# Parts of 16, 12 and 16 chunks in the channel mixers, norm blocks split inside the fourth down panel, and one moved set of seven products, in a two-layer hybrid decoder on one Trainium2 core

## The chip, the cores and the metric

The kernel runs on one core of one Trainium2 chip. The metric is the device time of one execution in microseconds (us); lower is better. The core has a matrix engine (TensorE, in the profile PE, its weight loads PEld), a vector engine (VectorE, DVE), a scalar engine (ScalarE, ACT), a general engine (GpSimd, POOL) and an engine for loads and waits (SyncE, SP). Each runs its own instructions in order, and they meet through semaphores. Transfers between main memory and the core's memory are issued by an engine into a queue and land later. TensorE accumulates into eight banks of 128 x 512 fp32.

## The reference: what is computed

256 tokens of width 2048 pass two layers. Each layer is a mixer (layer 0: gated linear attention, layer 1: forgetting attention, "FoX"; both with attention to 256 memory tokens beside it) and then a gated MLP, the channel mixer, with a causal depthwise convolution of width 3:

```python
def conv_ffn(h, w_up, conv_w, conv_b, w_down):      # w_up 2048 x 11264, w_down 5632 x 2048
    u = causal_dwconv(h @ w_up, conv_w, conv_b)
    a, val = split_cols(u, [FFN_HIDDEN, FFN_HIDDEN])
    return (jax.nn.silu(a) * val) @ w_down

for i in range(2):
    if i == 1:
        fk, fv, fc = fox_shared_kv(x, fox_kv_norm, fox_w_kv, fox_b_f)   # rmsnorm(x) @ w_kv
    h = rmsnorm(x, norm_mix[i]);  x = x + mixer_i(h, ...)
    h = rmsnorm(x, norm_ffn[i]);  x = x + conv_ffn(h, ...)
return rmsnorm(x, norm_final)
```

All of it is fp32. The FoX keys and values are made from the residual stream after layer 0's channel mixer, so the step after that channel mixer is a norm and a product with the key weights.

## The kernel before

**Products.** Each fp32 operand is held as a high and a low part (fp32r), and a product takes three matmuls: high x high, high x low, low x high. Activations are stored as chunks of 128 features by 256 tokens with both parts. Weights come as units of 128 x 1024 fp32 (512 KB): SP loads a unit into one of four `raw` buffers, ACT casts it to the high part `whi` (L229) and VectorE subtracts to get the low part `wlo` (L230), each with four buffers. A plain unit then costs TensorE twelve matmuls of 512 columns.

**Sets of seven.** In `pair_steps` (L379) two neighbouring chunks k, k+1, two halves of the tokens and two halves of the columns form a 2 x 2 block product. For chosen k it is done with seven products in place of eight (21 matmuls for 24). It needs sums of weight halves (VectorE, L425 to L428; casts at L375 and L376), sums of activations (`token_sums`, tiles `usum` and `dsum`), four more accumulator banks, and afterwards `early`, which adds the shared products to their places.

**The channel mixer** (`ffn`, L1363). The 5632 hidden features are 44 chunks. An up pair makes four of them: 16 units, one per chunk of the input `h`, with one set of seven at unit 6 (`SEVEN_UP`), and in some pairs another at 11 (`SEVEN_MORE`). Its results are scaled, transposed on VectorE, sent to main memory and brought back transposed through GpSimd's queue (`far_away`, L629), and then go through convolution taps on ACT (L1381), additions on VectorE (L1388), silu (L1394), the product (L1401) and the split into high and low part (L513, L514), which give the chunk `m`. `m` is a ring of 20 chunks. After each part of the chunks (`PARTS`) the down panels of that part run: a wide panel for columns 0 to 1023 (f = 0) and one for 1024 to 2047 (f = 2), one unit per chunk; they add into the residual stream x. In the last part only the first panel is wide; the columns from 1024 on are two panels of 512, f = 2 and f = 3 (`panel_tm`, L312, in layer 0, `rows_tm`, L343, in layer 1), two chunks per unit. Below they are the third and the fourth panel.

**Order.** The work behind an up pair waits in a list. After each unit, `tick` gives it a credit (1.3, 1.7 or 2.1), and the steps whose turn has come are issued until the credit is used up: half a credit a tap, one an addition. Results return three ticks after they were sent, and their taps begin eight ticks after. A planner then orders each engine's instructions by a simulated time: what is ready goes, loads and casts with priority over the rest, and `issue_after` sets what an instruction may not come ahead of. So a step written late can stand earlier in an engine's queue.

**After the last part.** When a panel of x is done, `then(f, b)` (L1588) adds up its squares (ACT, L608) and transposes the block (VectorE, L1594); with both token halves there, the block is sent away on GpSimd's queue. `land` (L1572) brings it back with four transfers, and `take` (L1581) splits it with the norm gain into four chunks of the next input, with ACT (L524) and VectorE (L526). In layer 0 these four blocks are the input of the FoX keys, and `fox` (L1132) starts with `two_tm`: six units of key panel 0, six of key panel 1, then the last two of each. Unit u of a key panel reads chunks 2u and 2u + 1, so units 0 and 1 need block 0, units 2 and 3 block 1, and so on. In the code before, the first block is taken at the end of the fourth panel and the others inside the key panels:

```python
for u in (4, 5):
    f2(u)
    then.land()
for u in range(2, 6):
    if u == 5:
        then.land()
        then.take()
    f3(u)
```

In layer 1 `then` (L1653) multiplies x with the gain of the last norm (L1657, `gf`, loaded by SP in `begin`), and `last` (L1659) ends the kernel: it adds the fourth panel to x, computes the root and writes out, for token half 0 and then half 1. Its last weight units are kept in `spare` tiles, so that half 1 needs no second load.

Of the kernel before, what the change touches and what calls it, by code (L numbers as in the profile page):

```python
# [13 lines left out]
F32 = mybir.dt.float32  # L14
# [6 lines left out]
P = 128  # L21
# [8 lines left out]
RANK = 16  # L30
TAU = 16.0
BIG = 1e30
PARTS = ((0, 16), (16, 32), (32, 44))
RING = 20
SEVEN_UP = (6,)
SEVEN_DOWN = (4, 10)
SEVEN_MORE = 11


# [106 lines left out]
def _trunk(ctx: ExitStack, tc: tile.TileContext, xt, xtok, memt, wp, wgu, gns, gfin, cnv, par, msk, out):  # L146
# [196 lines left out]
    def rows_tm(key, src, evac):  # L343

        units = where[key]
        n = units[0][2]
        base = min(min(u[1]) for u in units)
        acc = [pacc.tile([P, 512], F32, name="acc", tag="acc") for _ in range(2)]
        end = len(units) - 1
        ready = {}  # L350

        def step(i, blocks=(0, 1), hold=None):
            if i not in ready:
                ready[i] = split_unit(units[i]) if hold is None else split_apart(units[i], hold)
            for low in range(2):
                for b in blocks:
                    for j, kc in enumerate(units[i][1]):
                        w = ready[i][low]
                        w = w[j] if isinstance(w, list) else w[:, j * n : (j + 1) * n]
                        for part in range(2 - low):  # L360
                            mm = TE.matmul(acc[b][:, :n], src[kc - base][:, part, b * P : (b + 1) * P], w, start=i == low == part == j == 0,  # L361
                                           stop=i == end and low == 1 and j == len(units[i][1]) - 1)
# [769 lines left out]
    def fox(nx, vt, stash):  # L1132
        hk, hq, mix = bufB, bufA, bufB
        with (
# [24 lines left out]
            def query_input(i):  # L1159
                split_turned(hq, i, (*stash, spare[1])[i // 4], "mix1")  # L1160

            two_tm([fk(0), fk(1)], 8, 2, {(0, 0): nx.take, (0, 3): nx.take, (1, 2): nx.row,
                                          (1, 3): lambda: nx.land(spare[1]), (1, 5): nx.take})
            step = fk(2)
            for u in range(8):
# [197 lines left out]
    def ffn(l, nx, h, m, ys, zs, landing, then, pool, temps, last=None, spare=None):  # L1363
        with tc.tile_pool(name=f"ffn{l}", bufs=1) as fp:
# [8 lines left out]
            def held(name, i):  # L1373
                return fp.tile([P, 2, 4, P], F32R, name=name, tag=f"{name}{i}")
# [21 lines left out]
            def gated(j, s):  # L1396

                if s == 0:
                    product[0] = fp.tile([P, 2, T], F32, name="cv", tag="cv")
                    with tc.issue_after(lows[-1].ins):  # L1400
                        V.tensor_tensor(product[0], taps[0][:, :, 0, :], taps[0][:, :, 1, :], ALU.mult)  # L1401
                r = product[0]
                with tc.issue_after(lows[-1].ins):
                    split(m, (j + s) % RING, r[:, s, :])
                    if s and j < PARTS[-1][0] and j % 16 in SEVEN_DOWN:
                        sums[j] = held("dsum", j % 16)
                        token_sums(r, sums[j])

            product = [None]
# [89 lines left out]
            for p, (lo, hi) in enumerate(PARTS[:-1]):  # L1499
# [10 lines left out]
                more = {SEVEN_MORE: input_sums(SEVEN_MORE, "dsum", SEVEN_DOWN[0])}  # L1510
            lo, hi = PARTS[-1]
            while done < hi:
                drive(up_pair(done, more), 1.3 if done + 4 < hi else 1.7)
                more = {}
                done += 4
            p = len(PARTS) - 1
            src = [m[c % RING] for c in range(lo, hi)]
            wide = down_pair(l, p, 0, src, {}, 0, pool, lambda: (temps(0), temps(1)), then)

            def third(b, a):  # L1520
                add_to(2)(b, a)
# [2 lines left out]
            if l:  # L1524
                f2, f3 = [rows_tm(("down", l, p, f), src, evac) for f, evac in ((2, third), (3, last))]
            else:
                for f, k in zip((2, 3), SEVEN_DOWN):
                    then.rooms[f] = lambda k=k: fp.tile([P, 4, 4, 2, 32], F32, name="tblk", tag=f"dsum{k}")
                f2 = panel_tm(("down", l, p, 2), src, third)
                f3 = panel_tm(("down", l, p, 3), src, lambda b, a: (add_to(3)(b, a), then(3, b)))  # L1530
            for k in range(8):
                next(wide)
                tick(1.7)
            getattr(then, "begin", int)()
            for step, n in ((f2, 4), (f3, 2)):
                for u in range(n):
                    step(u)
                    tick(2.1)
            if l:
# [66 lines left out]
    n = gla(nx)  # L1606
# [159 lines left out]
```

## Time and profile before

| | us |
|---|---|
| median of 3 runs | 2234.88 (2233.97 to 2235.39) |
| the profiled execution | 2235.35 |
| its span | 2233.6 |
| TensorE busy in it | 2212.0 |
| VectorE busy | 1779.7 |
| ACT busy | 1418.3 |
| GpSimd busy | 136.1 |

The granted clock of TensorE in that execution is 0.998 of full speed. The lengths of matmuls in a profile overlap, since they are pipelined, so the pace of TensorE is read from start to start. In a row of a timeline stand the start, the length, the engine, the line, the operation, what it writes and reads, the count of merged instructions, and in brackets the idle time of the engine before it with what ended that. Names of tiles can be those of an earlier owner of the same place: for layer 0 `B` is the input of the up pairs and later of the FoX keys, and `mix`, `A` and `more...` are chunks of m.

### The profile page before, as it was taken

What the parts mean: (1) busy time and instruction counts of PE and PEld (TensorE: products, weight loads), DVE (VectorE), ACT (ScalarE), POOL (GpSimd) and SP (SyncE); (2) the same over time, 40 slices, a digit from 0 to 9 for tenths busy, and PEclk for the clock granted to TensorE, in tenths of its full rate; (3) what the DMA queues carried; (4) which work ended last, traced back from release to release, by engine and by line L of the source; (5) the groups of instructions that cost most, each with busy time, mean ns of one, the idle gap of its engine ahead of it and who ended that gap; (6) DMA issues with size and microseconds to landing.
All of it is one profiled execution on the core that took longest, in us unless ns stands there. A gap on an engine that the chain in (4) does not pass through costs nothing.

```text
span 2233.6 us, 30036 instructions
## 1 busy us (share of the span) xinstructions
PE 2212.0 (99%) x10323; PEld 1852.3 (83%) x10323; DVE 1779.7 (80%) x2638; ACT 1418.3 (63%) x2255; POOL 136.1 (6%) x257
## 2 busy tenths in 40 slices
PE   9999999999999999999999999999999999999998
PEld 7888888888788888888877998888878888888886
DVE  7768977688887888888867559668898788978876
ACT  6655664556786567665665455455787647676466
POOL 0000000001100001100111000000100000110010
PEclk9999999999999999999999999999999999999999
DMA  9867667877678567766677867777677757765674
GB/s 349 248 223 226 192 188 243 249 240 239 227 237 255 193 220 250 222 229 212 227 236 248 236 200 243 225 244 242 220 234 238 244 198 234 258 228 209 224 236 165
DMA packets 165633, 515.47 MB, mean 231 GB/s; under 512 B 20700, under 2 KB 41832, under 8 KB 165480
## 3 DMA queue, kind: packets, MB, share of 16 engines
q1 hardware_dynamic: 148488, 461.36, 63.2%
q0 software_dynamic: 16416, 51.40, 7.6%
q8 instruction: 81, 1.33, 0.2%
q10 hardware_dynamic: 576, 0.79, 0.1%
q14 instruction: 72, 0.59, 0.1%
HBM read 469.68 MB, written 43.79 MB: 230 GB/s over the span
## 4 chain that ended last, share of the span: by engine, by line
PE 91%; ACT 3%; issue 2%; DMA 2%; DVE 0%; POOL 0%; SPq 0%; ACTq 0%; DVEq 0%; POOLq 0%
PE acc L400 27%; PE acc L333 23%; PE ps_s L400 14%; PE ps_o L400 7%; PE ps_t L400 7%; PE acc L305 3%; PE acc L260 3%; PE ps_s L333 2%; DMA fvt<-far 2%; PE acc L258 1%; ACT tap L1381 1%; ACT whi L229 1%; PE acc L361 1%; PE ps_s L1008 0%; ACT whi L375 0%
## 5 line engine op out<-in xcount | busy, mean ns | idle before, releaser
L230 DVE TENSOR_TENSOR wlo<-raw,whi 128x1024 fp32r<-128x1024 f32 (+4 forms) x739 | 874.3, 1193 | 295.6 <-ACT whi L229 278.1
L229 ACT ACTIVATE whi<-raw 128x1024 fp32r<-128x1024 f32 (+4 forms) x739 | 760.9, 1037 | 443.1 <-PE acc L333 157.9
L333 PE MATMUL acc<-whi,B 128*128 128x512 f32 (+3 forms) x1248 | 294.8, 371 | 5.7 <-ACT B L524 5.7
L333 PEld LDWEIGHTS acc<-whi,B 128*128 128x128 f32 x1248 | 227.7, 189 | 34.8 <-ACT B L524 6.5
L375 ACT ACTIVATE whi<-raw 128x1024 fp32r<-128x1024 f32 (+1 forms) x136 | 129.9, 955 | 195.5 <-PE acc L400 71.7
L400 PE MATMUL acc<-whi,B 128*128 128x512 f32 x794 | 203.1, 390 | 1.4 <-ACT whi L229 1.3
L376 DVE TENSOR_TENSOR wlo<-raw,whi 128x1024 fp32r<-128x1024 f32 (+1 forms) x136 | 147.8, 1088 | 69.9 <-ACT whi L375 61.3
L400 PE MATMUL acc<-whi,mix 128*128 128x512 f32 x754 | 192.6, 390 | 1.2 <-ACT whi L229 1.0
L400 PEld LDWEIGHTS acc<-whi,B 128*128 128x128 f32 x794 | 148.6, 188 | 34.3 <-ACT whi L229 3.3
L400 PEld LDWEIGHTS acc<-whi,mix 128*128 128x128 f32 x754 | 141.2, 188 | 32.6 <-ACT whi L229 2.8
L333 PE MATMUL acc<-wlo,B 128*128 128x512 f32 (+3 forms) x624 | 159.5, 369 | 0.0
L1381 ACT ACTIVATE tap<-yzu,cw 128x256 f32<-128x256 f32 x264 | 124.8, 532 | 5.5 <-DMA yzu<-far 5.1
L1381 ACT ACTIVATE tap<-fvt,cw 128x256 f32<-128x256 f32 x264 | 124.4, 529 | 6.0 <-DMA fvt<-far 6.0
L333 PEld LDWEIGHTS acc<-wlo,B 128*128 128x128 f32 x624 | 114.7, 188 | 14.6
L1388 DVE TENSOR_TENSOR tap<-tap,tap 128x1024 f32<-128x1024 f32 x88 | 106.7, 1213 | 20.6 <-ACT tap L1381 20.6
L400 PE MATMUL acc<-wlo,B 128*128 128x512 f32 x397 | 112.3, 390 | 0.0
L400 PE MATMUL ps_s<-whi,mix 128*128 128x512 f32 x394 | 107.3, 389 | 0.0
L400 PE MATMUL acc<-wlo,mix 128*128 128x512 f32 x377 | 106.6, 390 | 0.0
L400 PE MATMUL ps_s<-whi,B 128*128 128x512 f32 x342 | 94.2, 389 | 0.0
L400 PEld LDWEIGHTS acc<-wlo,B 128*128 128x128 f32 x397 | 74.4, 188 | 16.0 <-DVE wlo L230 0.5
L400 PEld LDWEIGHTS ps_s<-whi,mix 128*128 128x128 f32 x394 | 74.0, 188 | 15.7
L400 PEld LDWEIGHTS acc<-wlo,mix 128*128 128x128 f32 x377 | 70.6, 188 | 15.2 <-DVE wlo L230 0.5
(490 smaller groups left out, 3752.8 us busy)
## 6 DMA issues: line engine op xcount, KB each, us to landing
raw<-wp SPq DMA_DIRECT2D x743, 512.0 KB, 4.6
fvt<-far POOLq DMA_DIRECT2D x100, 128.0 KB, 5.5
raw<-wp SPq DMA_DIRECT2D x32, 384.0 KB, 3.7
far<-yu POOLq DMA_DIRECT2D x22, 512.0 KB, 5.8
far<-yzu POOLq DMA_DIRECT2D x22, 512.0 KB, 5.7
yzu<-far POOLq DMA_DIRECT2D x88, 128.0 KB, 5.2
raw<-wp SPq DMA_DIRECT2D x24, 388.0 KB, 4.6
x<-xtok SPq DMA_DIRECT2D x8, 512.0 KB, 7.3
```

Of the source, the lines that this page charges most:

```text
L229: casts.append(S.activation(hi[:, s], raw[:, s], AF.Copy))
L230: lows.append(V.tensor_tensor(lo[:, s], raw[:, s], hi[:, s].bitcast(F32), ALU.subtract))
L258: mm = TE.matmul(acc[p][c][:, :T], w[:, s], both[:, 0, :], start=False, stop=end and j == 3)
L260: mm = TE.matmul(acc[p][c], w[:, s], both, start=u == j == 0, stop=end and j == 3)
L305: mm = TE.matmul(acc[b][:, :n], src[kcs[j] - base][:, part, b * P : (b + 1) * P], w, start=u == 0 and low == part == j == 0, stop=u == end ...
L333: mm = TE.matmul(acc[b][:, :n], src[kc - base][:, part, b * P : (b + 1) * P], ready[low][:, j * n : (j + 1) * n], start=i == low == part = ...
L361: mm = TE.matmul(acc[b][:, :n], src[kc - base][:, part, b * P : (b + 1) * P], w, start=i == low == part == j == 0, stop=i == end and low = ...
L375: casts.append(S.activation(hi[:, :n], src, AF.Copy))
L376: lows.append(V.tensor_tensor(lo[:, :n], src, hi[:, :n].bitcast(F32), ALU.subtract))
L400: r = TE.matmul(bank[name], x, w, start=name not in begun, stop=last)
L1381: S.activation(by_run(taps[i][:, s, c, i:]), zs[slot][:, :, 2 * c + s], AF.Copy if i else AF.Identity, bias=0.0 if i else w[3], scale=w[2 ...
L1388: V.tensor_tensor(taps[0], taps[0], taps[n][:, :, :, :T], ALU.add)
```

## The change

- The parts are of 16, 12 and 16 chunks (before 16, 16 and 12).
- The down panels use sets of seven at chunks 4 and 10 (part 1), 20 (part 2) and 32 (part 3, in the wide panel); before at 4, 10 (part 1) and 20, 26 (part 2). The sums' two buffers get new names.
- The last up pair has the credit 1.3 (before 1.7).
- In the last part twelve units of the wide panel run first (before eight) with the credit 2.1 (before 1.7), then three units of the third panel (before four of the third and two of the fourth, in layer 1 also two half units), then the wide panel's last four, then what is left of the third and the fourth panel: 5 and 8 units (before 2 and 4).
- In layer 0 blocks 0, 1 and 2 are landed and taken inside the third and fourth panel; in the key panels two takes fall away.
- In layer 1 units 4 to 7 of the fourth panel run for token half 0 and then for half 1, with `spare` tiles for 4 and 5.
- `rows_tm` takes its accumulators at its first unit.

```diff
-PARTS = ((0, 16), (16, 32), (32, 44))
+PARTS = ((0, 16), (16, 28), (28, 44))
-SEVEN_DOWN = (4, 10)
+SEVEN_DOWN = {4: 0, 10: 1, 20: 0, 32: 1}
...
-        acc = [pacc.tile([P, 512], F32, name="acc", tag="acc") for _ in range(2)]
+        acc = []
...
         def step(i, blocks=(0, 1), hold=None):
+            if not acc:
+                acc.extend(pacc.tile([P, 512], F32, name="acc", tag="acc") for _ in range(2))
...
-            two_tm([fk(0), fk(1)], 8, 2, {(0, 0): nx.take, (0, 3): nx.take, (1, 2): nx.row,
+            two_tm([fk(0), fk(1)], 8, 2, {(1, 2): nx.row,
                                           (1, 3): lambda: nx.land(spare[1]), (1, 5): nx.take})
...
-                    if s and j < PARTS[-1][0] and j % 16 in SEVEN_DOWN:
-                        sums[j] = held("dsum", j % 16)
+                    if s and j in SEVEN_DOWN:
+                        sums[j] = held("dsum", SEVEN_DOWN[j])
                         token_sums(r, sums[j])
...
-                drive(up_pair(done, more), 1.3 if done + 4 < hi else 1.7)
+                drive(up_pair(done, more))
...
-            wide = down_pair(l, p, 0, src, {}, 0, pool, lambda: (temps(0), temps(1)), then)
+            wide = down_pair(l, p, 0, src, {c - lo: t for c, t in sums.items()}, 0, pool, lambda: (temps(0), temps(1)), then)
...
-            for k in range(8):
+            last_pair = hi - lo - 4
+            for k in range(last_pair):
                 next(wide)
-                tick(1.7)
+                tick(2.1)
             getattr(then, "begin", int)()
-            for step, n in ((f2, 4), (f3, 2)):
-                for u in range(n):
-                    step(u)
-                    tick(2.1)
-            if l:
-                for u in (2, 3):
-                    f3(u, (0,), spare)
-                    tick(1.0)
+            for u in range(3):
+                f2(u)
+                tick(2.1)
             for _ in wide:
                 tick(2.1)
             assert not waiting and not returns
             if l:
-                for u in (4, 5):
+                for u in range(3, 8):
                     f2(u)
+                for u in range(4):
+                    f3(u)
                 for b in range(2):
-                    for u in range(2 if b else 4, 6):
-                        f3(u, (b,))
+                    for u in range(4, 8):
+                        f3(u, (b,), spare if u < 6 else None)
             else:
-                for u in (4, 5):
-                    f2(u)
-                    then.land()
-                for u in range(2, 6):
-                    if u == 5:
-                        then.land()
-                        then.take()
-                    f3(u)
+                hooks = {(2, 3): then.land, (2, 5): then.land, (2, 7): then.take, (3, 1): then.take, (3, 2): then.land,
+                         (3, 5): then.take}
+                for f, step, at in ((2, f2, 3), (3, f3, 0)):
+                    for u in range(at, 8):
+                        step(u)
+                        hooks.get((f, u), int)()
```

More of the change, by code (lines that the diff above doesn't have):

```diff
@@ L1509, in ffn @@
                 sums.clear()
-                more = {SEVEN_MORE: input_sums(SEVEN_MORE, "dsum", SEVEN_DOWN[0])}
+                more = {SEVEN_MORE: input_sums(SEVEN_MORE, "dsum", 0)}
             lo, hi = PARTS[-1]
             while done < hi:
-                drive(up_pair(done, more), 1.3 if done + 4 < hi else 1.7)
+                drive(up_pair(done, more))
                 more = {}
@@ L1526, in ffn @@
             else:
-                for f, k in zip((2, 3), SEVEN_DOWN):
+                for f, k in ((2, 0), (3, 1)):
                     then.rooms[f] = lambda k=k: fp.tile([P, 4, 4, 2, 32], F32, name="tblk", tag=f"dsum{k}")
```

## The prediction

> **What bounds the kernel now.** I read the page first, then the waits of TensorE, then its timeline around each gap, then the queues of ACT, GpSimd and VectorE at the places the change touches.
>
> ```profile
> span 2233.6 us, 30036 instructions
> ...
> PE 2212.0 (99%) x10323; PEld 1852.3 (83%) x10323; DVE 1779.7 (80%) x2638; ACT 1418.3 (63%) x2255; POOL 136.1 (6%) x257
> ```
>
> TensorE is busy for 2212.0 of 2233.6 us, so 21.6 us of idle time is all that a change of order can work on, plus what a busy row hides. The waits of TensorE (us in total, times, longest) say where the movable part is:
>
> ```profile
> PE acc L333 <- ACT B L524: 5.7, 2, 4.8
> PE acc L400 <- ACT whi L229: 2.2, 4, 0.9
> ...
> PE acc L333 <- ACT whi L229: 1.1, 1, 1.1
> ```
>
> The rest of the idle time is the start and the tail after the last matmul. The timeline of TensorE (start, length, what, count) shows these waits in place:
>
> ```profile
> 1085.32 2.11 PE L400 MATMUL acc<-whi,B 128*128 128x512 f32 x8 [0.87 <-ACT whi L229]
> ...
> 1133.07 2.11 PE L333 MATMUL acc<-whi,moremk 128*128 128x512 f32 x8 [1.12 <-ACT whi L229]
> ...
> 1165.84 1.98 PE L333 MATMUL acc<-whi,mix 128*128 128x512 f32 x8
> ...
> 1168.56 1.98 PE L333 MATMUL acc<-whi,mix 128*128 128x512 f32 x8
> ...
> 1170.37 1.07 PE L333 MATMUL acc<-wlo,mix 128*128 128x512 f32 x4
> 1176.22 3.30 PE L333 MATMUL acc<-whi,B 128*128 128x512 f32 x7 [4.78 <-ACT B L524]
> 1179.36 0.62 PE L333 MATMUL acc<-wlo,B 128*128 128x512 f32 x2
> ...
> 1182.77 0.61 PE L333 MATMUL acc<-wlo,B 128*128 128x512 f32 x2
> 1184.28 1.89 PE L333 MATMUL acc<-whi,B 128*128 128x512 f32 x7 [0.90 <-ACT B L524]
> 1186.01 0.62 PE L333 MATMUL acc<-wlo,B 128*128 128x512 f32 x2
> ...
> 2138.23 2.10 PE L400 MATMUL acc<-whi,mix 128*128 128x512 f32 x8 [0.59 <-ACT whi L229]
> ```
>
> From 1165.84 to 1168.56 one unit of twelve matmuls takes 2.72 us, 0.227 us each: that is the pace, and the lengths shown overlap. At that pace the first FoX key unit was due at 1170.37 + 4 x 0.227 = 1171.28. It came at 1176.22, 4.94 us late. Its first seven matmuls then took 3.14 us (1176.22 to 1179.36) in place of 1.59, another 1.55. The second wait costs 1184.28 - (1182.77 + 0.45) = 1.06 and 0.14 in the seven after it. The entry into the FoX keys thus costs 7.7 us: it waits for the splits (L524) of the norm blocks.
>
> **The change part by part.** TensorE's work does not change. In both versions a layer has eleven up pairs with one set of seven products each, two pairs with one more, and four sets in the down panels (two, two, none before; two, one, one after), and each chunk passes the same panels. Term: 0.
>
> *Norm blocks in the fourth panel.* Before, five units (13.6 us, 1157.68 to 1171.28) lay between the end of the wide last down panel and the FoX keys, since the planner had drawn one unit forward. After, it is five units of the third panel and eight of the fourth, 13 x 2.72 = 35.4 us. The queues of GpSimd and ACT:
>
> ```profile
> 1159.87 0.56 POOL L632 DMA_DIRECT2D far<-blk  x1 [28.96 <-DVE blk L1594]
> ...
> 1166.60 2.21 POOL L637 DMA_DIRECT2D fvt<-far  x4
> ...
> 1179.05 2.17 POOL L637 DMA_DIRECT2D fvt<-far  x4 [5.28 <-DMA far<-tblk]
> ```
>
> ```profile
> 1175.66 1.70 ACT L524 ACTIVATE B<-fvt,gains 128x256 fp32r<-128x256 f32 x4 [3.34 <-DMA fvt<-far]
> ...
> 1183.72 1.71 ACT L524 ACTIVATE B<-fvt,gains 128x256 fp32r<-128x256 f32 x4 [2.19 <-DMA fvt<-far]
> ...
> 1187.88 1.69 ACT L524 ACTIVATE B<-fvt,gains 128x256 fp32r<-128x256 f32 x4
> ```
>
> Counted from 1157.68, block 0 could be split at +18.0 and block 1 at +26.0 us. Block 2 was split at 1187.88, 27.5 us after its panel ended at 1160.40. After the change they are needed at +35.4, +40.8 and +46.2 us, and block 2's panel ends at +13.6, so it comes at +41.1. All three are in time, by 17, 15 and 5 us. Block 3 stays where it was, behind twelve units of keys. The entry stall goes: **-7.7 us**. What is late next there is a cast, not a block.
>
> The price is a new wait inside the fourth panel. The three splits now stand on ACT among the weight casts of that panel, and a block that is not there yet holds the casts. What that costs is seen in the wide panel before:
>
> ```profile
> 1120.19 1.06 ACT L229 ACTIVATE whi<-raw 128x1024 fp32r<-128x1024 f32 x1 [1.66 <-PE ps_t L400]
> 1126.78 5.28 ACT L1381 ACTIVATE tap<-fvt,cw 128x256 f32<-128x256 f32 x12 [5.53 <-DMA fvt<-far]
> 1131.97 2.94 ACT L229 ACTIVATE whi<-raw 128x1024 fp32r<-128x1024 f32 x3
> ```
>
> ACT stood 5.53 us and worked 5.28 us on taps, and TensorE lost only the 1.12 us at 1133.07, because the four weight buffers put the casts three units ahead: 3 x 2.72 - 1.06 = 7.1 us of cover. A split of a block takes 1.70 us, so with the same 5.5 us of waiting it holds ACT for 7.2, which the cover about hides; with the 3.34 us of 1175.66 it hides it fully. Two waits inside one cover (5.5 + 1.7 + 2.2 + 1.7 = 11.1) would show 4.0 us, and a third some 2 more. Bounds 0 to +6 us; I take **+1.5**, nearer the single wait, since two units lie between the first two splits and four before the third. The lands are issued on GpSimd (2.21 us for the four returns of a block at 1166.60), which then has only the blocks' own transfers in its queue; what waits behind a land there is the next block's send, and SP's loads are not in that queue. The eight VectorE halves of each split move along and fit in 35.4 us.
>
> ```profile
> far<-yu POOLq DMA_DIRECT2D x22, 512.0 KB, 5.8
> ...
> fvt<-far POOLq DMA_DIRECT2D x100, 128.0 KB, 5.5
> ```
>
> These are the two legs, 5.8 and 5.5 us, 11.3 in a row. The Trainium skill (DMA: Bandwidth & Descriptors, Anatomy of one DMA - SWDGE (gpsimd) path) fits a GpSimd-issued transfer as 2.0 us plus bytes over 436 GB/s: as an estimate from that page, 3.2 and 2.3 us, 5.5 in all. By it the blocks would land before ACT reaches their splits, the term would be 0 and the sum 1.5 us lower; the trace's legs are twice as long, so I stay with them. The Trainium skill (TensorE: Matmul & The Clock Gate, Architectural detail) also calls ACT's queue strict FIFO, which speaks against this change; the trace agrees at 1131.97, where three casts ran only behind the taps.
>
> *A set of seven in the wide panel, twelve of its units first, credit 2.1.* The set of chunk 26 in part 1 becomes one of chunk 32 in the last part's first panel. For the before this panel is light:
>
> ```profile
> 974.00:1017.00 43.00, 43.00 (x190) 35.44 (x189) 40.64 (x53) 22.65 (x26) 0.00 (x0) 1.00 0.58 203
> 1104.60:1157.70 53.10, 51.98 (x230) 42.72 (x229) 37.52 (x44) 33.07 (x54) 5.47 (x10) 1.00 0.73 238
> ```
>
> ```profile
> L230 DVE TENSOR_TENSOR wlo<-raw,whi 128x1024 fp32r<-128x1024 f32 x673 | 811.7, 1217 | 250.0 <-ACT whi L229 239.2 <-PE acc L258 2.7 <-issue 2.7
> L376 DVE TENSOR_TENSOR wlo<-raw,whi 128x1024 fp32r<-128x1024 f32 x102 | 124.7, 1222 | 55.6 <-ACT whi L375 52.4 <-PE acc L400 1.7
> ...
> L425 DVE TENSOR_TENSOR raw<-raw 128x512 f32<-128x512 f32 x34 | 23.4, 688 | 0.6
> ...
> L376 DVE TENSOR_TENSOR wlo<-raw,whi 128x512 fp32r<-128x512 f32 x34 | 23.2, 683 | 14.4 <-ACT whi L375 8.9 <-PE ps_t L400 5.5
> ...
> L483 DVE TENSOR_TENSOR x<-x,acc 128x512 f32<-128x512 f32 x36 | 23.6, 678 | 2.6 <-PE acc L333 2.5
> ```
>
> In a window the third busy time is VectorE's: 37.52 of 53.10 us from the start of the wide panel to its end. A set costs VectorE 0.683 + 3 x 1.222 + 4 x 0.688 = 7.1 us in place of two units' 2.4, and its early sums some 7 x 0.68 = 4.8. That makes 37.5 + 9.5 = 47.0, and the stretch after is fourteen plain units, one set (21 x 0.227 = 4.8) and three units of the third panel, 51.0 us: 92%. The down panel with two sets at 974 to 1017 has 40.64 of 43.00, 94%, and no wait of TensorE in it. So there is room, but less for a late transfer. The tap wait of 1126.78 can stay, go (-1.4, the 1.12 and some 0.3 around it) or grow to 3 us a layer. Bounds -1.4 to +6 for both layers; I take **+1.0**, near the 94% row.
>
> *Credit 1.3 in place of 1.7 in the last up pair.* The waits at 1085.32 and 2138.23 lie in that pair, 1.2 and 0.9 us with their ramps. Less work drawn into it may remove them (-2.1), its place as third pair after a down may keep them. Bounds -2.1 to +1; I take **0**, because the third pair of a layer has a wait today with credit 1.3, at 568.10 in layer 0:
>
> ```profile
> 568.10 2.11 PE L400 MATMUL acc<-whi,B 128*128 128x512 f32 x8 [0.39 <-ACT whi L229]
> ```
>
> *Part 1 with twelve chunks, its one set, the two buffers with new names, accumulators taken late.* They lie beside TensorE in panels without a wait (the 974 row is the densest): 0; if that cover went, the price is that of the wide panel. *The norm gains of layer 1* are loaded on SP's queue, now behind twelve units; nineteen us (seven units) remain to their use: 0.
>
> *The tail of layer 1.* The last units still give block 0 and then block 1 of rows, four half units (24 x 0.227 = 5.4 us) apart, now with four loads in a row ahead of them; their buffers are filled ahead: 0.
>
> ```profile
> 2218.75 0.62 PE L361 MATMUL acc<-wlo,mix 128*128 128x512 f32 x2
> ...
> 2223.36 0.61 PE L361 MATMUL acc<-wlo,mix 128*128 128x512 f32 x2
> ```
>
> ```profile
> 2220.29 0.74 DVE L1667 TENSOR_TENSOR x<-x,acc 128x256 f32<-128x256 f32 x2
> ...
> 2224.59 0.75 DVE L1667 TENSOR_TENSOR x<-x,acc 128x256 f32<-128x256 f32 x2
> ```
>
> TensorE ends the row blocks at 2219.37 and 2223.97; VectorE takes them up 0.92 and 0.62 us later, since it is still on the norm of the third and first panels. These end 12 to 15 units earlier after the change, so the last block is taken up at once: **-0.6**, bounds -0.6 to 0.
>
> **The sum.** -7.7 + 1.5 + 1.0 + 0 - 0.6 = -5.8 us. The profiled execution took 2235.35 us (its span is 2233.6, 1.75 lie around it), 0.47 above the median of 2234.88; on the median the sum gives **2229.1 us**. With all low ends it is -11.8, 2223.1; with all high ends +5.3, 2240.2. What a measurement of this kernel can tell from no change is about 0.2%, 4.5 us: 2230.4 and 2239.3.
>
> **Rivals.** *The blocks hold ACT.* The waits of the three splits add up: +6 in place of 1.5. For it: ACT waited for such blocks by 3.34 and 2.19 us, for taps by 5.53. Against it: 7.1 us of cover each time. 2234.88 - 7.7 + 6 + 1.0 - 0.6 = 2233.6. The change would then not have removed the stall but moved it one panel forward. If a single gap passes some length, TensorE restarts slowly, as at 1176.22 (+1.55); the gaps of 1.12 and 0.87 had no such ramp. The Trainium skill (TensorE: Matmul & The Clock Gate, Part 1) puts that length at an idle window of about 3.4 us, after which the clock is halved; the trace agrees, with 4.78 above and 1.12 below it.
>
> *The wide panel starves.* With a set of seven and its casts in the panel, ACT and VectorE no longer recover from a late tap transfer. Now the hold of 5.53 + 5.28 us costs 1.1 because three units are cast ahead; with one unit ahead (2.72 us) it costs 5.53 + 5.28 + 1.06 - 2.72 = 9.2 a layer. It decides from (5.8 + 4.5 + 1.0) / 2 = 5.7 us a layer on: then the kernel is slower. At 7 us a layer: -5.8 - 1.0 + 14 = +7.2, 2242.1. For it: 92% of VectorE. Against it: the up pairs, which hold a set and taps at once, lose 0.9 at most.
>
> *Every wait goes.* The wide panel's and the last pair's waits vanish with the entry's: 2223.1. For it: the lighter credit of the last pair; against it: the wait at 568.10, with that credit.
>
> **How the numbers follow.** The forecast, 2225 to 2230.4, gets 0.42; every wait gone 0.08; the blocks hold ACT 0.30; the wide panel starves 0.20. Faster by over 0.2% is the first two, 0.50; within 0.2% the third, 0.30; slower the last, 0.20. The range 2224.5 to 2237.5 holds the forecast and the held ACT and leaves out the worst of the starved panel and the best case.
>
> **What would show it.** Right: no wait of L333 on L524 at the entry, the key units at once at 0.227 us a matmul, and splits of L524 on ACT some 10 us before it. The held ACT would show as waits of L333 or of a cast inside the fourth panel, behind L524 with a transfer as releaser. The starved panel would show as waits of L400 on ACT or VectorE between the last up pair and the third panel, in both layers. The tail would show L1667 within 0.2 us of the last matmul. The prediction is wrong if the planner places the splits ahead of many casts, or if the wide panel's taps come later than their 22 us.

## The result, and the profile after

The changed kernel takes 2232.68 us in the median (2229.52 to 2234.66), the kernel before 2235.07 (2232.98 to 2238.54) beside it: a ratio of 0.9986, with a 95% interval of 0.998 to 0.9993. That is 2.4 us less, 0.14%: small, inside the 0.2% that the prediction takes for no change, though the interval leaves out 1. The profiled execution took 2230.85 us, 1.8 below its own median. In the changed kernel most lines have numbers two higher: the matmuls of L400 stand at L402, the casts of L375 at L377, the splits of L524 at L526.

The page of the changed kernel, its span and busy times:

```profile
span 2229.1 us, 30049 instructions
...
PE 2211.6 (99%) x10323; PEld 1851.9 (83%) x10323; DVE 1789.9 (80%) x2654; ACT 1418.9 (64%) x2257; POOL 136.0 (6%) x257
```

TensorE is busy for 0.4 us less than before (2212.0), so 4.1 of the 4.5 us between the spans are idle time. The waits of TensorE in the changed kernel (total, times, longest):

```profile
PE acc L402 <- ACT whi L377: 4.4, 4, 1.2
...
PE acc L402 <- ACT whi L229: 1.2, 3, 0.4
PE acc L402 <- DVE wlo L378: 0.7, 2, 0.3
```

The wait of L333 on the splits (5.7 us) is gone, and a wait that was not there has come: four times for the casts L377 and twice for L378, which belong to sets of seven. The timeline of TensorE shows where:

```profile
1094.72 0.40 PE L402 MATMUL ps_s<-wlo,dsum 128*128 128x512 f32 x1
1096.28 1.20 PE L402 MATMUL acc<-whi,dsum 128*128 128x512 f32 x4 [1.16 <-ACT whi L377]
1097.79 0.73 PE L402 MATMUL acc<-wlo,dsum 128*128 128x512 f32 x2 [0.32 <-DVE wlo L378]
1099.55 0.73 PE L402 MATMUL acc<-whi,dsum 128*128 128x512 f32 x2 [1.02 <-ACT whi L377]
1100.11 0.63 PE L402 MATMUL ps_s<-whi,A 128*128 128x512 f32 x2
...
1170.59 1.09 PE L333 MATMUL acc<-whi,mix 128*128 128x512 f32 x4
...
1171.98 1.99 PE L333 MATMUL acc<-whi,B 128*128 128x512 f32 x8
...
1870.07 2.14 PE L402 MATMUL acc<-whi,mix 128*128 128x512 f32 x8 [0.41 <-ACT whi L229]
...
2143.41 1.19 PE L402 MATMUL acc<-whi,dsum 128*128 128x512 f32 x4 [1.24 <-ACT whi L377]
```

At 1171.98 the FoX keys begin without a wait, and the tap wait (1.12 us at 1133.07 before) and the two waits of the last up pair (0.87 and 0.59) are gone. From 1094.72 to 1100.11 nine matmuls take 5.39 us in place of 9 x 0.227 = 2.04: the set of seven that moved into the last part costs 3.4 us a layer, 6.8 in all. That is more than its three waits (2.50 us), since the starts of the matmuls around them are also further apart than the pace.

What holds its cast is seen in the queues of ACT and of VectorE at that place:

```profile
1092.53 0.73 ACT L515 ACTIVATE moremv<-cv 128x256 fp32r<-128x256 f32 x2 [3.97 <-DVE cv L1403]
1094.68 0.60 ACT L1321 ACTIVATE fvt<-acc 128x512 f32<-128x512 f32 x1 [1.42 <-PE acc L402]
1095.17 1.05 ACT L377 ACTIVATE whi<-raw 128x1024 fp32r<-128x1024 f32 x1
1098.44 1.06 ACT L377 ACTIVATE whi<-raw 128x1024 fp32r<-128x1024 f32 x1 [2.21 <-DVE raw L430]
```

```profile
1093.35 0.68 DVE L428 TENSOR_TENSOR raw<-raw,raw 128x512 f32<-128x512 f32 x1
...
1095.31 0.69 DVE L485 TENSOR_TENSOR x<-x,fvt 128x512 f32<-128x512 f32 x1 [0.94 <-ACT fvt L1321]
1095.92 0.68 DVE L429 TENSOR_TENSOR raw<-raw,raw 128x512 f32<-128x512 f32 x1
```

The data of the third cast are ready at 1094.03 (L428, 1093.35 + 0.68). But ACT has the copy L1321 ahead of it, which stands in `early` and takes a finished accumulator of the set to `fvt`; it waits 1.42 us for TensorE, and the cast runs at 1095.17, 1.14 us late. On VectorE the addition of that copy to x (L485) waits 0.94 us for it, ahead of the subtractions L429 and L430 that the fourth cast needs. TensorE waits for casts that stand behind a copy of TensorE's own result.

In the kernel before, the same copy (there L1319) stands behind the last cast of the set (there L375), so it holds none of them. ACT at the second of its two sets in a panel:

```profile
1001.90 1.06 ACT L375 ACTIVATE whi<-raw 128x1024 fp32r<-128x1024 f32 x1 [1.98 <-DVE raw L428]
...
1003.90 0.57 ACT L1319 ACTIVATE fvt<-ps_o 128x512 f32<-128x512 f32 x1
```

The splits of the norm blocks in the fourth panel, in ACT's queue:

```profile
1157.00 1.71 ACT L526 ACTIVATE B<-fvt,gains 128x256 fp32r<-128x256 f32 x4 [3.71 <-DMA fvt<-far]
...
1162.69 1.31 ACT L526 ACTIVATE B<-fvt,gains 128x256 fp32r<-128x256 f32 x3 [3.04 <-DMA fvt<-far]
...
1169.47 1.71 ACT L526 ACTIVATE B<-fvt,gains 128x256 fp32r<-128x256 f32 x4 [0.62 <-DMA fvt<-far]
1171.08 1.69 ACT L526 ACTIVATE mix<-fvt,gains 128x256 fp32r<-128x256 f32 x4
```

ACT stood 3.71, 3.04 and 0.62 us for the blocks, and TensorE did not notice it in this execution. The rows that write `mix` are splits of the same block for the query input; the planner put them there too.

The end, VectorE's addition of the last row block:

```profile
2220.04 0.75 DVE L1665 TENSOR_TENSOR x<-x,acc 128x256 f32<-128x256 f32 x2 [1.16 <-PE acc L363]
```

TensorE's last record begins at 2219.39 and is 0.61 long, so it ends at 2220.00, and VectorE takes the block up 0.04 us later. Before it was 0.62 us.

### The profile page after: what moved, and what is told of

Same layout as the page of the kernel before. It is cut to its first block, busy times and chain, and to the rows that moved or that the text cites. A ratio compares the mean times of both kernels' runs of the same rounds, so it can differ in the third digit from the quotient of the medians.

```text
span 2229.1 us, 30049 instructions
## 1 busy us (share of the span) xinstructions
PE 2211.6 (99%) x10323; PEld 1851.9 (83%) x10323; DVE 1789.9 (80%) x2654; ACT 1418.9 (64%) x2257; POOL 136.0 (6%) x257
## 4 chain that ended last, share of the span: by engine, by line
PE 90%; issue 5%; ACT 2%; DMA 1%; DVE 1%; POOL 0%; SPq 0%; ACTq 0%; DVEq 0%; POOLq 0%
PE acc L333 26%; PE acc L402 25%; PE ps_s L402 13%; PE ps_o L402 7%; PE ps_t L402 6%; PE acc L305 3%; PE acc L260 3%; PE acc L363 2%; PE ps_s L333 2%; PE acc L258 1%; ACT tap L1383 1%; DMA raw<-wp 1%; ACT whi L229 1%; PE ps_s L1010 0%; DMA yzu<-far 0%
## 5 line engine op out<-in xcount | busy, mean ns | idle before, releaser
L333 PE MATMUL acc<-whi,B 128*128 128x512 f32 (+3 forms) x1248 | 291.8, 370 | 0.0
L333 PEld LDWEIGHTS acc<-whi,B 128*128 128x128 f32 x1248 | 227.1, 188 | 28.1
L377 ACT ACTIVATE whi<-raw 128x1024 fp32r<-128x1024 f32 (+1 forms) x136 | 129.7, 954 | 188.8 <-PE ps_t L402 76.4
L378 DVE TENSOR_TENSOR wlo<-raw,whi 128x1024 fp32r<-128x1024 f32 (+1 forms) x136 | 147.6, 1087 | 65.5 <-ACT whi L377 60.7
L402 PE MATMUL acc<-whi,mix 128*128 128x512 f32 x764 | 195.4, 390 | 0.9 <-ACT whi L229 0.8
L402 PE MATMUL acc<-whi,B 128*128 128x512 f32 x750 | 193.0, 390 | 0.5 <-ACT whi L229 0.4
L402 PEld LDWEIGHTS acc<-whi,mix 128*128 128x128 f32 x764 | 143.0, 188 | 32.5 <-ACT whi L229 2.5
L402 PEld LDWEIGHTS acc<-whi,B 128*128 128x128 f32 x750 | 140.6, 188 | 31.0 <-ACT whi L229 1.6
L333 PE MATMUL acc<-wlo,B 128*128 128x512 f32 (+3 forms) x624 | 158.6, 369 | 0.0
L333 PEld LDWEIGHTS acc<-wlo,B 128*128 128x128 f32 x624 | 114.5, 188 | 14.6 <-DVE wlo L230 0.2
L402 PE MATMUL acc<-wlo,mix 128*128 128x512 f32 x382 | 107.8, 390 | 0.0
L402 PE MATMUL acc<-wlo,B 128*128 128x512 f32 x375 | 107.1, 390 | 0.0
L402 PE MATMUL ps_s<-whi,mix 128*128 128x512 f32 x386 | 105.2, 389 | 0.0
L402 PE MATMUL ps_s<-whi,B 128*128 128x512 f32 x342 | 94.3, 390 | 0.0
L402 PEld LDWEIGHTS ps_s<-whi,mix 128*128 128x128 f32 x386 | 72.5, 188 | 15.3
L402 PEld LDWEIGHTS acc<-wlo,mix 128*128 128x128 f32 x382 | 71.6, 188 | 15.3 <-DVE wlo L230 0.3
L402 PEld LDWEIGHTS acc<-wlo,B 128*128 128x128 f32 x375 | 70.3, 188 | 15.0 <-DVE wlo L230 0.3
```

The costliest lines, as they stand in the source:

```text
L377: casts.append(S.activation(hi[:, :n], src, AF.Copy))
L378: lows.append(V.tensor_tensor(lo[:, :n], src, hi[:, :n].bitcast(F32), ALU.subtract))
L402: r = TE.matmul(bank[name], x, w, start=name not in begun, stop=last)
```

## The experiments

All ratios are against the kernel before, run beside them. The question was first why the moved set costs 6.8 us, and then why the median gained 2.4 and not the 4.5 us of the spans.

**The changed kernel once more**, with no edit.

> The changed kernel once more, unchanged, since its runs spread from 2229.5 to 2234.7 us while its profiled execution of 2230.85 lies near the lower end. If the spread comes from the splits of the norm blocks, which hold ACT for 3.7 and 3.0 us in the profiled execution without a wait of TensorE, another profiled execution near 2233 shows waits of TensorE on ACT in the third or fourth panel of layer 0 of 1 to 3 us. If it comes from somewhere else, the new wait is at another place, and the splits again cost nothing. In every execution the waits inside the set of seven of the wide panel stay, some 2.5 us of idle time a layer.

2231.98 us (2230.83 to 2235.31), ratio 0.9989, 0.998 to 0.9998. The set's waits are the same to 0.1 us. The profiled execution, 1.8 us longer, has other waits in the fourth panel and behind it (TensorE, then ACT):

```profile
1170.21 0.74 PE L333 MATMUL acc<-wlo,mix 128*128 128x512 f32 x2 [0.63 <-DVE wlo L230]
...
1176.46 2.14 PE L333 MATMUL acc<-whi,B 128*128 128x512 f32 x8 [1.38 <-ACT whi L229]
```

```profile
1162.87 1.31 ACT L526 ACTIVATE B<-fvt,gains 128x256 fp32r<-128x256 f32 x3 [3.95 <-DMA fvt<-far]
...
1172.16 1.71 ACT L526 ACTIVATE B<-fvt,gains 128x256 fp32r<-128x256 f32 x4 [3.13 <-DMA fvt<-far]
...
1175.37 1.99 ACT L229 ACTIVATE whi<-raw 128x1024 fp32r<-128x1024 f32 x2
```

The third block's splits came 2.7 us later than at 1169.47, and the casts at 1175.37 stood behind them. So the splits in the fourth panel cost nothing in one execution and 0.63 + 1.38 = 2.0 us of waits in another, by when the blocks land. Measured from start to start against the pace, with the matmuls right behind the waits, it is 2.6 us.

**The set at another place.** Two kernels move it: to chunk 24, as second set in the part of twelve chunks (called part 1 in places, counted from 0), and to chunk 36, four units later in the last part.

```diff
-SEVEN_DOWN = {4: 0, 10: 1, 20: 0, 32: 1}
+SEVEN_DOWN = {4: 0, 10: 1, 20: 0, 24: 1}
```

> The changed kernel with the set of seven of chunk 32 (wide panel of the last part) back in part 1, at chunk 24. Theory A, VectorE is full when the set's subtractions come, because the last up pair's results, their transposes and the tap additions stand before them: the three waits inside the set go, 3.4 us a layer with their ramps, and nothing new comes: 2232.7 - 6.8 = about 2226 us. Theory B, the last up pair's late results and taps hold the wide panel whatever stands in it: the waits move to a plain unit of the wide panel, 2 to 3 us a layer stay, 2231 to 2233 us.

```diff
-SEVEN_DOWN = {4: 0, 10: 1, 20: 0, 32: 1}
+SEVEN_DOWN = {4: 0, 10: 1, 20: 0, 36: 1}
```

> The changed kernel with the wide panel's set four chunks later, at chunk 36 (its ninth and tenth unit) in place of chunk 32 (its fifth and sixth). Theory A (VectorE is full at the start of the panel): by then the transposes are over, and most of the 3.4 us a layer go: 2226 to 2229 us. Theory C, ACT's copy for the early sums (L1321), which waits for the first shared product, stands in ACT's queue ahead of the set's third cast and holds it wherever the set is: the waits at the set stay at 1 us or more each, 2232 to 2233 us.

The first, chunk 24: 2230.53 us (2228.4 to 2231.66), ratio 0.9975, 0.9966 to 0.9984. That lies between what was expected if VectorE was too full there (2226) and if the waits stayed in the wide panel (2231 to 2233), and neither happened: the last part's wide panel has no wait, but the set waits at its new place, 946.14 and 947.67, by 1.16 and 0.35 us (in layer 1 by 1.17 and 0.34). ACT there:

```profile
944.54 0.60 ACT L1321 ACTIVATE fvt<-acc 128x512 f32<-128x512 f32 x1 [2.48 <-PE acc L402]
945.04 1.05 ACT L377 ACTIVATE whi<-raw 128x1024 fp32r<-128x1024 f32 x1
```

Chunk 36: 2229.83 us (2228.94 to 2231.47), ratio 0.9975, 0.9964 to 0.9985. This too lies between the two expected ranges. Of the set's waits one of 0.98 us is left in layer 0, for a cast behind nine taps, and none in layer 1; the copy L1321 stands behind the casts in this order. Besides, the profiled execution has four waits in and behind the key panels, 2.8 us together. So the waits belong neither to the last part nor to the stretch behind its last up pair. At both places where a set waits 1.16 us, chunks 32 and 24, the copy is ahead of its cast.

**Less work drawn beside the set.**

```diff
-                tick(2.1)
+                tick(1.3 if k < 6 else 2.1)
```

> The changed kernel with the credit 1.3 in place of 2.1 in the first six units of the wide panel, so that less of the list (tap additions, silu, product) is drawn ahead of the set of seven. Theory A: one tap addition (1.2 us) and the product and split (1.5 us) fall behind the set, so the waits inside it shrink by 1 to 2.7 us a layer: 2228 to 2231 us. Theory C (ACT's copy ahead of the third cast): no change, 2232 to 2233 us. If the planner orders by readiness alone, whatever the credit, no change either.

2231.31 us (2229.45 to 2234.5), ratio 0.9981, 0.9973 to 0.999. The first wait of the set is unchanged, 1.16; the second (0.32) is gone and the third falls from 1.02 to 0.35, so the waits sum to 1.51 us where they had 2.50. VectorE in this kernel:

```profile
1093.24 0.69 DVE L429 TENSOR_TENSOR raw<-raw,raw 128x512 f32<-128x512 f32 x1
1095.29 0.69 DVE L485 TENSOR_TENSOR x<-x,fvt 128x512 f32<-128x512 f32 x1 [1.36 <-ACT fvt L1321]
```

VectorE has time to spare and stands for the copy: its load is not what makes the first cast late. It has a part in the later ones, which shrank with less work beside them.

**The copy behind the casts.** This undoes the suspected cause alone, in `early`.

```diff
-            S.activation(t0, bank["p1"], AF.Copy)
+            with tc.issue_after(casts[-1].ins):
+                S.activation(t0, bank["p1"], AF.Copy)
```

> The changed kernel with ACT's copy of the first shared product in a down panel's early sums (L1321) issued behind the set's last cast. In the profiled executions so far that copy stands ahead of the set's third cast and waits for TensorE, while the cast's data are ready 0.6 to 1.1 us before it. Theory C (the copy holds the cast): the first of the waits inside the set shrinks from 1.2 us to under 0.3, and the sum of the set's waits from 2.5 to about 1 us a layer; 2232.4 - 3 = about 2229.5 us. Theory A (VectorE's subtractions are late): the waits stay at 2 us a layer or more, 2232 us.

2227.55 us (2225.66 to 2230.51), ratio 0.9967, 0.9956 to 0.9979, which lies below the changed kernel's whole interval. In the medians that is 7.4 us against before where the change had 2.4. TensorE and ACT:

```profile
1094.48 0.40 PE L402 MATMUL ps_s<-wlo,dsum 128*128 128x512 f32 x1
1095.21 1.20 PE L402 MATMUL acc<-whi,dsum 128*128 128x512 f32 x4 [0.34 <-ACT whi L377]
1096.88 0.73 PE L402 MATMUL acc<-whi,dsum 128*128 128x512 f32 x2 [0.46 <-ACT whi L377]
1097.44 0.63 PE L402 MATMUL ps_s<-whi,A 128*128 128x512 f32 x2
```

```profile
1094.10 1.06 ACT L377 ACTIVATE whi<-raw 128x1024 fp32r<-128x1024 f32 x1 [0.90 <-DVE raw L428]
1095.77 1.06 ACT L377 ACTIVATE whi<-raw 128x1024 fp32r<-128x1024 f32 x1 [0.60 <-DVE raw L430]
...
1098.63 0.58 ACT L1322 ACTIVATE fvt<-acc 128x512 f32<-128x512 f32 x1
```

The third cast runs when its data are there, 1094.10, and the set has 0.80 us of waits in layer 0 and 0.97 in layer 1, where it had 2.50 and 2.59. Against the pace seven matmuls take 2.96 us from 1094.48 to 1097.44 in place of 1.59: the set costs 1.4 us, and 1.5 in layer 1, 2.9 in all where it cost 6.8. So the copy's place is worth 3.9 us; the medians moved by 5, and what the rest is was not traced. What is left at the set are casts that wait for VectorE's sums: ACT stood 0.90 us for L428 and 0.60 for L430. This kernel is better than both. The same line in the kernel before:

> The kernel before with the copy behind the set's casts and nothing else. Its profiled execution has no wait inside a set of seven (no TensorE wait on L375), so theory C expects no gain: 2235 us within 1.5 us. A gain of 2 us or more would mean that the copy holds casts there too, in time that the waits do not show.

2235.27 us (2233.1 to 2236.2), ratio 1.0, 0.9991 to 1.0009: there the copy is behind the casts already, so there is nothing to win, and the wait at the entry remains, 5.94 us. With the set at chunk 24 and at chunk 36:

> The changed kernel with the set back in part 1 (chunk 24) and the copy behind the set's casts. With the set in part 1 the last of its two sets had the same wait of 1.16 and 0.35 us, with the copy ahead of the third cast. Theory C: these go as they went in the wide panel, 2230.5 - 2 to 3 = 2227.5 to 2228.5 us, no better than the set in the wide panel with the copy behind. Theory A (VectorE in the wide panel): a free wide panel is worth more than that, 2226 or less.

> The changed kernel with the set four chunks later (chunk 36) and the copy behind the set's casts. With the set at chunk 36 one wait of 1.0 us was left in layer 0, behind a run of nine taps that stands ahead of the third cast, and the copy was already behind the casts. Theory C therefore expects nothing from the copy's place here: 2229.8 within 1 us. If it gains 2 us or more, the copy also acted in part 1 or in the up pairs.

2227.29 us (2225.96 to 2230.1), ratio 0.9966, 0.9953 to 0.9978, with 0.25 us of waits left in the set at chunk 24; and 2229.35 us (2227.85 to 2233.02), ratio 0.9979, 0.997 to 0.9987, no gain over chunk 36 alone, where the copy was behind already. With the copy in its place, chunk 24 and chunk 32 give the same time.

**The norm blocks as before, the rest as after.** Block 0 is split at the end of the fourth panel, blocks 1 and 2 inside the key panels.

```diff
-            two_tm([fk(0), fk(1)], 8, 2, {(1, 2): nx.row,
+            two_tm([fk(0), fk(1)], 8, 2, {(0, 0): nx.take, (0, 3): nx.take, (1, 2): nx.row,
...
-                hooks = {(2, 3): then.land, (2, 5): then.land, (2, 7): then.take, (3, 1): then.take, (3, 2): then.land,
-                         (3, 5): then.take}
+                hooks = {(2, 3): then.land, (2, 5): then.land, (3, 2): then.land, (3, 7): then.take}
```

> The changed kernel with the splits of the norm blocks where they were: block 0 split behind the fourth panel's last unit, blocks 1 and 2 in the key panels after their units 0 and 3; the landings stay inside the third and fourth panel. If the longer stretch between the wide panel and the keys (13 units) is what removed the entry's stall, and the place of the splits only decides how long ACT is held, the entry stays without a wait for a block, and the time is that of the changed kernel within 2 us: 2231 to 2234. If the early splits removed it, TensorE waits again for ACT's splits at the first key unit, 1.7 us of ACT and 2.2 us of VectorE work at least: 2234 to 2237 us.

2235.12 us (2231.84 to 2241.22), ratio 1.0003, 0.9994 to 1.0012: 2.4 us more than the changed kernel, and the two intervals just miss each other. By its time it lies where it was expected to lie if the early splits had removed the stall (2234 to 2237), yet no wait for a block came back. ACT in its fourth panel:

```profile
1163.32 1.31 ACT L526 ACTIVATE mix<-fvt,gains 128x256 fp32r<-128x256 f32 x3 [7.71 <-DMA fvt<-far]
```

The planner put the query input's splits of the same blocks there, which nothing binds to a unit, and ACT stood 7.71 us in a row. TensorE then waited 1.60 us for a cast at 1176.07, and 1.54 us at 1201.47 behind VectorE (L593). So it is the distance between the panels that removes the entry's wait. A wait like the 1.60 us also came with the places of the change (1.38 in the second execution); that the longer hold of ACT makes the 2.4 us is not shown.

**Later splits.** With the copy behind the casts, the three blocks are split after units 5 and 7 of the fourth panel and after the first key unit.

```diff
-            two_tm([fk(0), fk(1)], 8, 2, {(1, 2): nx.row,
+            two_tm([fk(0), fk(1)], 8, 2, {(0, 0): nx.take, (1, 2): nx.row,
...
-                hooks = {(2, 3): then.land, (2, 5): then.land, (2, 7): then.take, (3, 1): then.take, (3, 2): then.land,
-                         (3, 5): then.take}
+                hooks = {(2, 3): then.land, (2, 5): then.land, (3, 2): then.land, (3, 5): then.take, (3, 7): then.take}
```

> The kernel with the copy behind the set's casts, and besides the splits of the norm blocks later: block 0 after unit 5 of the fourth panel, block 1 after its last, block 2 after the first key unit. If the waits left around the end of the fourth panel (0.9 us at 1168.84, in other executions up to 2.0 us) come from ACT and VectorE standing at a split whose block has not landed, they go, and the spread of the runs with them: 2226 to 2227.5 us. If the later splits bring a wait at the key units for a block or for the casts behind it, 2228.5 to 2231 us.

2228.95 us (2227.92 to 2233.28), ratio 0.9977, 0.9968 to 0.9986: no better than with the places of the change. Its longest execution is the profiled one, with a wait of 3.19 us at 1176.68 for a cast; ACT stood 5.50 us there for the third block. A later split holds the casts as well.

**The set alone in the kernel before** (chunk 26's set moved to chunk 36, in its wide panel, with the accumulators taken late).

```diff
-SEVEN_DOWN = (4, 10)
+SEVEN_DOWN = {4: 0, 10: 1, 20: 0, 36: 1}
...
```

> The kernel before with one part of the change alone: the set of seven of chunk 26 in part 1 moves into the wide panel of the last part (chunk 36, its fifth and sixth unit), and the narrow panels of layer 1 take their accumulators at their first unit, as the changed kernel does. Everything else is as before. If the set in that panel is by itself what costs, 2 to 3.4 us a layer come on top: 2235.1 + 4 to 7 = 2239 to 2242 us. If it costs only together with the higher credit or the shorter part 1, the time stays within 1.5 us of before.

2244.8 us (2243.66 to 2246.72), ratio 1.0046, 1.0033 to 1.0058: 9.9 us slower, more than expected. The set waits 0.47 + 0.32 + 1.01 us a layer, behind L1321 once more (ACT waits 2.65 us for TensorE at 1116.42). From start to start that is 2.7 us a layer, as expected. Unexpected is the entry, which grew:

```profile
1179.58 3.35 PE L333 MATMUL acc<-whi,B 128*128 128x512 f32 x7 [7.59 <-ACT B L526]
...
1188.20 0.73 PE L333 MATMUL acc<-whi,B 128*128 128x512 f32 x2 [1.09 <-ACT B L526]
...
1196.12 1.75 PE L333 MATMUL acc<-whi,B 128*128 128x512 f32 x7
```

Four key units, due at 1171.83, are through at 1196.12: 24.3 us for 48 matmuls, 13.4 more than at the pace, where before had 7.7. Why the blocks come later in this order was not tried.

**The credit of the last up pair.**

```diff
-                drive(up_pair(done, more))
+                drive(up_pair(done, more), 1.3 if done + 4 < hi else 1.7)
```

> The changed kernel with the credit of the last up pair back at 1.7. In the profiled execution before, that pair had a wait of 0.87 us in layer 0 and 0.59 in layer 1, 2.1 us with their ramps; in the changed kernel it has none. If the credit drew the work that caused them, they come back: 2232.4 + 2.1 = 2234.5 us. If the shift of the pair to another place after the down panels removed them, nothing changes: 2232.4 within 1 us. If the higher credit empties the list before the wide panel's set and so frees VectorE there, the set's waits shrink and the time falls to 2230 or less.

2235.55 us (2233.2 to 2237.07), ratio 0.9997, 0.9988 to 1.0006, 2.9 us above the changed kernel; the two intervals overlap, so the trace has to carry it. The waits of the last pair did not come back, so it was not the lower credit that removed them. The set's waits grew:

```profile
1096.55 1.20 PE L402 MATMUL acc<-whi,dsum 128*128 128x512 f32 x4 [1.77 <-ACT whi L377]
1098.75 1.22 PE L402 MATMUL acc<-whi,dsum 128*128 128x512 f32 x2 [0.99 <-ACT whi L377]
1099.77 1.05 PE L402 MATMUL ps_s<-whi,A 128*128 128x512 f32 x2
...
1102.24 0.62 PE L402 MATMUL ps_s<-whi,A 128*128 128x512 f32 x2
```

The eight matmuls from 1098.75 to 1102.24 take 3.49 us where 1.82 is the pace. The busy times by stretches (the figure behind POOL is the granted clock of TensorE):

```profile
1094.60:1098.75 4.15, 1.39 (x6) 0.68 (x5) 3.73 (x7) 3.01 (x6) 1.87 (x4) 1.00 0.22 79
1098.75:1102.24 3.49, 3.49 (x8) 2.78 (x9) 3.48 (x3) 3.49 (x7) 0.31 (x1) 0.52 0.46 129
```

The set costs 1.94 + 1.29 us until 1098.75 and 1.67 after it, 4.9 a layer against 3.4; twice the difference is 3.0, as large as the 2.9 us between the medians. The profiled execution also has a wait of 1.69 us at 1177.79, in the key units, where the two of the changed kernel have none and 1.38, so that the set alone makes the 2.9 us is likely and not shown. On ACT a split (L515, 0.71 us) now stands between the copy and the cast as well.

## Why the prediction was right or wrong

The direction was right and the time lies in the range; the gain was predicted as 5.8 us and measured as 2.4, and the time is 2.3 us above the forecast of 2225 to 2230.4. That it lies in the range is partly luck: the range was made wide enough for blocks that hold ACT, and the error of the wide panel (+4.4) was partly offset by the credit (-2.1) and, in one execution, by the splits (-1.5). In the profiled executions, by the prediction's steps and against the pace:

| step | predicted | profiled executions |
|---|---|---|
| entry into the FoX keys | -7.7 | -7.7 |
| splits in the fourth panel | +1.5 | 0, in another execution +2.6 |
| wide panel with a set of seven | +1.0 | -1.4 (tap wait) + 6.8 (set) = +5.4 |
| credit in the last up pair | 0 | -2.1 |
| tail of layer 1 | -0.6 | -0.6 |
| what was put at nothing | 0 | +0.7 (at 1870.07) |
| sum | -5.8 | -4.3, the spans differ by 4.5 |

*The entry* came out as worked: the keys at 1171.98 at once. The splits' order on ACT was not needed for that, as the kernel with the old places shows; the thirteen units between the panel and its consumer were.

*The splits* cost 0 and 2.6 us in the two executions, on both sides of the 1.5. Overlooked was that the query input's splits of the same blocks follow them, though ACT has them in the kernel before as well (L524 on `mix` at 1177.67 and 1185.33). The two legs that the prediction shows (5.8 and 5.5 us) are medians over rows that are mostly the up pairs'; the norm blocks' own sends stand in the trace of before with 4.2 and 7.4 us. No term was worked out from the legs.

*The wide panel* is the step that failed: taken as +1.0, it came as +5.4. The +1.0 was reached from the share of VectorE (92% against the 94% of a panel without a wait) and from a late tap transfer. The share does not tell it: with less work beside the set its first wait stayed at 1.16 us, and in part 1 the set waited as well. What decided was the order of ACT's queue, a copy that needs TensorE ahead of a cast that TensorE needs: 3.9 of the 6.8 us went when that order alone was changed. The 2.9 us that stay are casts that wait for VectorE's sums, so VectorE's work is the smaller part. The trace of before could have shown that the copy needs TensorE, but there it stands behind the casts; that the planner might put it ahead of them was not considered. The rival of the starved panel had the right place, near half its price (3.4 of 7 us a layer) and the wrong mechanism.

*The credit* was put at 0 between -2.1 and +1, and its low end is what came, but not by the credit: with 1.7 the pair's waits stay away too. What is left as a reason is the pair's place, now the fourth of its part where it was the third; that was not tried alone. What the low credit does is keep the set from costing another 3 us. The pattern of layer 0's third pair (0.39 us of wait there) did not carry over.

*The difference between 4.5 and 2.4 us* lies in which executions were profiled: that of before is 0.3 us above its median, that of the changed kernel 1.8 below. Of the two profiled executions of the changed kernel the longer one has the 2.6 us at the splits more and the wait at 1870 less. That the splits make up the spread of the others is not shown, since only these two executions have a trace.

The time of 2232.7 happens to lie near the 2233.6 of the rival in which the blocks hold ACT. It is not that rival: no execution showed its 6 us, and the copy in its place brings 5 us in the medians.

## What to carry to other kernels

Before a step is moved, look at each instruction that it puts into an in-order queue and ask what that one waits for: a set with a copy that waits for TensorE, planned ahead of a cast that TensorE needs next, cost 3.4 us with engines that were not full, and one line that binds the copy behind the casts took about 2 us of that away. A busy share says whether there is room, not whether the order fits. The round trip through memory was hidden here by distance: with thirteen units (35.4 us) between producer and consumer the wait for a block at the entry went, wherever the splits stood. What stays is that a split whose block has not landed holds the casts behind it, at no cost in one execution and for 3.19 us in another.

## What the runs showed of the hardware that was not expected

The prediction took gaps of about 1 us to be free of a slow restart, and only a long one (4.78 us) to be followed by it. In the kernel with credit 1.7 two gaps, 1.77 and 0.99 us with four matmuls between them, were followed by a granted clock of 0.52 over 3.49 us (the second row of its stretches above). In the kernel before with the set moved, gaps of 1.09 us at 1188.20 and 0.46 us at 1189.39 were enough; by then the clock was back at 1.00 from the low that followed the long gap before 1179.58. Its busy times by stretches, with the clock behind POOL:

```profile
1184.00:1188.00 4.00, 3.10 (x14) 2.25 (x12) 1.99 (x6) 2.37 (x3) 1.30 (x3) 1.00 0.91 277
1188.00:1192.00 4.00, 3.34 (x10) 2.39 (x11) 4.00 (x15) 4.00 (x11) 2.09 (x4) 0.79 0.78 266
1192.00:1196.00 4.00, 4.00 (x16) 3.20 (x15) 4.00 (x18) 3.21 (x8) 0.41 (x2) 0.79 0.43 122
```

The changed kernel kept the full clock around its set, with 2.50 us of waits in three gaps, in the same view from 1094 on:

```profile
1094.00:1098.00 4.00, 2.52 (x10) 1.45 (x9) 3.06 (x6) 1.54 (x2) 1.21 (x3) 1.00 0.30 114
1098.00:1102.00 4.00, 2.98 (x13) 2.01 (x13) 2.82 (x4) 3.56 (x4) 0.98 (x2) 1.00 0.49 131
```

So a drop came after 1.55 us of waits in two gaps and none after 2.50 us in three: neither the longest gap nor the sum decides alone, and short gaps close together can cost more than their length. The prediction's rule by a single long gap does not cover that. The Trainium skill (TensorE: Matmul & The Clock Gate, Part 1) describes a free-running activity window of about 3.4 us, so that the point of change depends on where in it the work falls. That would fit both cases, but no run here shows where the window stood.
